# Attention scores over 64 rows, with a PSUM bank for each head

## The chip, the cores and the metric

The kernel runs on one core of one Trainium2 chip. The metric is device time in microseconds (us). Three runs of the kernel before took 2879.69, 2884.32 and 2884.14 us; their median is 2884.14 us.

## The reference

Two layers of a backbone with 256 context tokens and 512 main tokens of width 1024. Each layer normalizes and modulates the tokens, projects them with `w_in`, passes the columns through four mixers of 256 channels each, gates and merges these, and ends in a mixture of experts. In the second layer the context tokens get no output. The change is in three of the mixers; each has 4 heads of 64 channels. Their cores, cut:

```python
# retention, in chunks of 128 tokens, in two directions
scores = einsum('bnihd,bnjhd->bnhij', qc, kc) * intra
o_intra = einsum('bnhij,bnjhe->bnihe', scores, vc)
o_cross = einsum('bnihd,hi,nbhde->bnihe', qc, q_dec, s_prev)

# neighborhood attention: blocks of 128 queries against 256 nearby and 256 context keys, one softmax
# window attention (GQA): blocks of 128 queries against up to 384 nearby and 256 context keys
s_w = where(valid, einsum('bqkgd,bskd->bkgqs', qb, kb), NEG)
s_c = einsum('bqkgd,bckd->bkgqc', qb, kc)
prob = softmax_with_sink(concatenate([s_w, s_c], -1), sink)
```

So every score is a sum over the 64 channels of one head.

## The kernel before

Tokens stand in tiles of 128 on the partitions. The large products (`product`, L560 to L562) are three fp32r matmuls for each 128 rows of weights (high times high, high times low, low times high), and their weights are streamed from memory and split by ScalarE (L436) and VectorE (L437). The mixers are Python generators. `tick` steps them from inside the large products, so that their instructions lie between those of the projections and gates; within that, the scheduler of the tile framework sets the order on each engine, and each engine then works through its list in that order. A mixer must be done when the merge comes to it (`finish`).

A pair p holds two heads, one in channels 0 to 63 and one in channels 64 to 127. Queries and keys are transposed so that the channels lie on the partitions. `pad_halves` (L640) evacuates the transposed queries twice: ScalarE writes head 0 into the lower half of one buffer (L653), VectorE head 1 into the upper half of another (L654), and GpSimd has filled the other halves with zeros (L643, L644). With these zeros a score is one matmul over all 128 rows of `kT`, and the other head's channels count nothing. The fp32 matmuls appear in the trace as two records each.

- `retention`: for each of 20 chunks (6 tiles and 4 tiles of the two layers, two pairs each) one matmul makes both heads' scores (L738, 256 columns), two the products with the state (L741, 128 columns each). VectorE applies mask and decay to both heads at once (L744, L746), adds the directions (L748), and two matmuls follow (L751), then the sum (L753).
- `ctx_attention`: 8 steps of the first layer; both heads' scores (L859) share one PSUM bank.
- `neighborhood`: 16 steps; for head 0 the window (L909) and the context scores (L910), the bias (L911), then the same for head 1.
- `gqa`: 16 steps; L984 makes the scores of 256 or 384 window keys, L987 the context scores, head after head. Where 384 + 256 columns exceed a bank of 512 (half of the steps) the context scores of both heads share a third bank.
- `attend` is what follows the scores in each of these 40 attention steps: the maxima (L794 or L799, L802), the exponentials with their sums (L809, and L812 for a sink), the reciprocal of the sum (L819), the scaling (L820 on ScalarE for head 0, L821 on VectorE for head 1), the transposes of the probabilities (L824), their evacuation (L830) and the products with the values (L841). L841 writes 64 output columns for each head, head 0 to the lower and head 1 to the upper partitions.

PSUM has 8 banks in four pools: `mm` 2, `sc` 3, `tr` 2, `mod` 1. Scores take `sc`; the transposes and L841 take `tr`.

Of the kernel before, what the change touches and what calls it, by code (L numbers as in the profile page):

```python
# [9 lines left out]
F32 = mybir.dt.float32  # L10
# [3 lines left out]
AF = mybir.ActivationFunctionType  # L14
OP = mybir.AluOpType
# [4 lines left out]
NCTX = 256  # L20
# [284 lines left out]
class Prog:  # L305
# [333 lines left out]

    def pad_halves(self, dst, scale, blocks=False):  # L640


        self.nc.gpsimd.memset(dst[0][64:128], 0.0)  # L643
        self.nc.gpsimd.memset(dst[1][0:64], 0.0)  # L644

        def f(ps, sl):
            lo, up = (scale, scale) if isinstance(scale, float) else (scale[0:64], scale[64:128])
            i0, i1 = ps[0:64], ps[64:128]
            o0, o1 = dst[0][0:64, sl], dst[1][64:128, sl]
            if blocks and sl.start >= NCTX:  # L650
                i0, i1 = (x.rearrange("p (r j c) -> p r j c", j=4, c=16) for x in (i0, i1))
                o0, o1 = (x.rearrange("p (j r c) -> p r j c", j=4, c=16) for x in (o0, o1))
            self.nc.scalar.activation(o0, i0, AF.Copy, scale=lo)  # L653
            self.nc.vector.tensor_scalar(o1, i1, up, None, op0=OP.mult)  # L654
        return f
# [30 lines left out]
    def retention(self, l, tiles, store):  # L686
# [4 lines left out]
        for p in range(2):  # L691
# [36 lines left out]
            self.rope(rq)  # L728
            qp = self.buf(128, 2, NTOK)
            evac = self.pad_halves([qp.v[:, h] for h in range(2)], 0.125)  # L730
            yield
# [24 lines left out]
            for b in (kT, qp, S):  # L756
                b.free()
# [91 lines left out]

    def ctx_attention(self, p, qp, kT, value, store, sink):  # L850

        nc = self.nc
        for t in range(2):
            sl = slice(t * 128, t * 128 + 128)

            def scores():
                sc = self.ps_sc.tile([128, 2, 256], F32, name="sc")
                for h in range(2):
                    nc.tensor.matmul(sc[:, h], qp[h][:, sl], kT.v[:, :NCTX], start=True, stop=True)  # L859
                return [[sc[:, h]] for h in range(2)]  # L860
            yield from self.attend(scores, lambda h, k: value(h, k),
                                   lambda yo: nc.scalar.dma_start(store[p * 128 : p * 128 + 128, sl], yo), sink)

    def neighborhood(self, l, tiles, store):
# [7 lines left out]
        for p in range(2):  # L872
# [15 lines left out]
            self.head_norm(nq.v)  # L888
            qs = [self.buf_old(128, NTOK) for _ in range(2)]
            qp = [b.v for b in qs]  # L890
            evac = self.pad_halves(qp, gain[:, 0:1], blocks=True)
            yield
# [3 lines left out]
            if t0 == 0:  # L896
                yield from self.ctx_attention(p, qp, kT, lambda h, k: nv.v[:, k, h * 64 : h * 64 + 64], store, None)
            for j in range(4):
# [5 lines left out]
                def scores():  # L904
                    out = []
                    for h in range(2):
                        q = qp[h][:, NCTX + j * 128 : NCTX + j * 128 + 128]
                        sc = self.ps_sc.tile([128, 512], F32, name="sc")
# [3 lines left out]
                        out.append([sc])  # L912
                    return out

# [7 lines left out]
                yield from self.attend(scores, value, put)  # L922
            for b in (nv, kT, *qs, vw):
                b.free()

    def gqa(self, l, tiles, store):
# [19 lines left out]
        for p in range(2):  # L946
# [13 lines left out]
            self.rope(q)  # L960
            qs = [self.buf_old(128, NTOK) for _ in range(2)]
            qp = [b.v for b in qs]
            evac = self.pad_halves(qp, 1.0)
            yield
# [5 lines left out]
            if t0 == 0:  # L970
                yield from self.ctx_attention(p, qp, kT, lambda h, k: val(k), store, sk)
            for n in range(4):
# [3 lines left out]

                def scores():
                    own = w + NCTX > 512
                    rest = self.ps_sc.tile([128, 2, 256], F32, name="sc") if own else None
                    out = []  # L980
                    for h in range(2):
                        qh = qp[h][:, sl]
                        sc = self.ps_sc.tile([128, 512], F32, name="sc")
                        nc.tensor.matmul(sc[:, :w], qh, kT.v[:, (keys[0] + 2) * 128 : (keys[-1] + 3) * 128],  # L984
                                         start=True, stop=True)
                        r = rest[:, h] if own else sc[:, w : w + NCTX]
                        nc.tensor.matmul(r, qh, kT.v[:, :NCTX], start=True, stop=True)  # L987
                        for i, m in enumerate(keys):
                            if m != n:
                                b = sc[:, i * 128 : i * 128 + 128]  # L990
                                nc.vector.tensor_tensor(b, b, self.c("band_l" if m < n else "band_r"), op=OP.add)
                        out.append([sc[:, :w], r] if own else [sc[:, : w + NCTX]])
# [6 lines left out]
            for b in (kT, *qs):  # L999
                b.free()  # L1000
# [1260 lines left out]
```

## Time and profile before

| | |
|---|---|
| median of three runs | 2884.14 us |
| the profiled execution | 2886.01 us, its span 2884.2 us |
| TensorE matmul busy | 2695.0 us (93%) |
| VectorE, ScalarE, GpSimd busy | 2080.1, 1462.2, 654.0 us |
| mean granted TensorE clock | 0.972 |
| where the mixers' scores lie in the span | first layer 339 to 722 us, second layer 1725 to 2092 us |

Busy time of TensorE includes the tail of each matmul that overlaps with the next one, so matmul durations are not added up; the distance from one start to the next is what a matmul costs in a stream. The gap from the profiled execution's 2886.01 us to its span is 1.8 us.

### The profile page before, as it was taken

The page shows a single profiled execution, that of the slowest core. Times are in us where ns is not written, and L with a number is a line of the kernel's source. Part 1 is how long each engine was busy: PE and PEld are TensorE (multiplying, and loading weights), DVE is VectorE, ACT ScalarE, POOL GpSimd, SP SyncE. Part 2 cuts the span into 40 slices and gives each one's busy share as a digit, 9 for nine tenths or more (in the row PEclk, how much of TensorE's full clock was granted, in tenths as well). Part 3 has the DMA queues.
Part 4 walks back from the last instruction along what each step waited for, and adds up shares of the span by engine and source line. Part 5 has one row for each costly group of instructions (what it writes and reads, how often), then busy time and mean ns, then how long its engine had stood idle before and what let it go on. Part 6 is the DMA issues. An engine that isn't in the chain of part 4 may idle for free. (4 is left out here: it accounts for less than half of the span.)

```text
span 2884.2 us, 39086 instructions
## 1 busy us (share of the span) xinstructions
PE 2695.0 (93%) x13190; PEld 1807.1 (63%) x13190; DVE 2080.1 (72%) x3921; ACT 1462.2 (51%) x2219; POOL 654.0 (23%) x596
## 2 busy tenths in 40 slices
PE   5999999999999699999997789999999699999998
PEld 2767666667678456666554467778788455555444
DVE  6754454647345989998886668755845999998887
ACT  4322342432132478887776434432233477776665
POOL 2231111001001441221111321021101543323332
PEclk8999999999999799999999899999999799999999
DMA  8687445243535799999997865365435899999994
GB/s 275 197 250 234 146 127 182 88 135 102 169 123 184 266 331 375 370 353 352 370 366 244 279 204 171 115 203 165 131 128 158 272 362 371 376 365 330 347 352 131
DMA packets 268646, 699.37 MB, mean 242 GB/s; under 512 B 64836, under 2 KB 83512, under 8 KB 268440
## 3 DMA queue, kind: packets, MB, share of 16 engines
q1 hardware_dynamic: 170672, 531.30, 51.8%
q0 software_dynamic: 39744, 113.86, 14.7%
q10 hardware_dynamic: 58024, 51.65, 5.7%
q8 instruction: 106, 1.74, 0.2%
q14 instruction: 100, 0.82, 0.1%
HBM read 622.48 MB, written 80.44 MB: 244 GB/s over the span
## 5 line engine op out<-in xcount | busy, mean ns | idle before, releaser
L437 DVE TENSOR_TENSOR big_r<-big,big_r 128x1024 fp32r<-128x1024 f32 x512 | 613.6, 1221 | 76.1 <-ACT big_r L436 69.0
L436 ACT CAST big_r<-big 128x1024 fp32r<-128x1024 f32 x517 | 532.5, 1051 | 150.6 <-PE mm L562 74.0
L560 PE MATMUL mm<-big_r,turned 128*128 128x512 f32 x1248 | 514.4, 412 | 10.3 <-ACT turned L436 6.6
L561 PE MATMUL mm<-big_r,turned 128*128 128x512 f32 x1248 | 504.7, 404 | 1.6 <-DVE big_r L437 1.5
L562 PE MATMUL mm<-big_r,turned 128*128 128x512 f32 x1248 | 504.5, 404 | 0.0
L437 DVE TENSOR_TENSOR big_r<-raw,big_r 128x1024 fp32r<-128x1024 f32 x392 | 464.0, 1216 | 41.4 <-ACT big_r L436 35.5
L436 ACT CAST big_r<-raw 128x1024 fp32r<-128x1024 f32 x395 | 402.9, 1049 | 66.6 <-PE sc L562 36.0
L561 PE MATMUL sc<-big_r 128*72 128x512 f32 (+1 forms) x1024 | 409.7, 400 | 19.6 <-DVE big_r L437 19.0
L560 PE MATMUL sc<-big_r 128*72 128x512 f32 (+1 forms) x1024 | 407.0, 398 | 0.0
L562 PE MATMUL sc<-big_r 128*72 128x512 f32 (+1 forms) x1024 | 404.9, 395 | 0.0
L560 PEld LDWEIGHTS mm<-big_r,turned 128*128 128x128 f32 x1248 | 236.9, 190 | 110.3 <-issue 41.1
L562 PEld LDWEIGHTS mm<-big_r,turned 128*128 128x128 f32 x1248 | 236.8, 190 | 57.3 <-issue 8.1
L561 PEld LDWEIGHTS mm<-big_r,turned 128*128 128x128 f32 x1248 | 237.3, 190 | 54.3 <-issue 6.5
L561 PEld LDWEIGHTS sc<-big_r 128*72 128x72 f32 (+1 forms) x1024 | 138.4, 135 | 139.0 <-DVE big_r L437 55.7
L1897 POOL DMA_INDIRECT out_dram<-big x32 | 162.2, 5068 | 266.2 <-DVE big L1874 261.9
L1866 PE MATMUL mm<-big_r 128*72 128x512 f32 (+1 forms) x512 | 204.0, 398 | 0.4 <-DVE big_r L437 0.2
L560 PEld LDWEIGHTS sc<-big_r 128*72 128x72 f32 (+1 forms) x1024 | 139.1, 136 | 100.7 <-ACT big_r L436 7.7
L1867 PE MATMUL mm<-big_r 128*72 128x512 f32 (+1 forms) x512 | 201.5, 393 | 0.0
L562 PEld LDWEIGHTS sc<-big_r 128*72 128x72 f32 (+1 forms) x1024 | 138.8, 136 | 85.6 <-issue 1.0
L1865 PE MATMUL mm<-big_r 128*72 128x512 f32 (+1 forms) x512 | 184.5, 394 | 1.1 <-DVE big L1874 0.6
L1382 ACT ACTIVATE wa<-mm 128x512 f32<-128x512 f32 x80 | 47.7, 596 | 239.9 <-PE mm L562 239.6
L1368 DVE SCALAR_TENSOR_TENSOR wa<-wa,mm 128x512 f32<-128x512 f32 x60 | 41.1, 685 | 147.2 <-PE mm L562 141.5
(381 smaller groups left out, 3794.0 us busy)
## 6 DMA issues: line engine op xcount, KB each, us to landing
big<-in_exp_w_dram SPq DMA_DIRECT2D x393, 512.0 KB, 7.5
raw<-in_exp_w_dram SPq DMA_DIRECT2D x375, 512.0 KB, 7.2
big<-in_mod_w_dram SPq DMA_DIRECT2D x96, 512.0 KB, 4.6
big<-in_w_in_dram SPq DMA_DIRECT2D x68, 512.0 KB, 5.5
big<-in_w_in_dram SPq DMA_DIRECT2D x48, 256.0 KB, 5.5
big<-s_wc POOLq DMA_DIRECT2D x16, 576.0 KB, 6.2
big<-s_ph POOLq DMA_DIRECT2D x16, 388.0 KB, 4.4
big<-s_wb POOLq DMA_DIRECT2D x16, 384.0 KB, 3.8
```

What stands on the lines that cost most here:

```text
L436: return (self.nc.scalar.copy(hi, src), (v or self.nc.vector).tensor_tensor(lo, src, hi.bitcast(F32), op=OP.subtract))
L437: (v or self.nc.vector).tensor_tensor(lo, src, hi.bitcast(F32), op=OP.subtract))
L560: nc.tensor.matmul(ps, ah, wh, start=(k == 0), stop=False)
L561: nc.tensor.matmul(ps, ah, wl, start=False, stop=False)
L562: nc.tensor.matmul(ps, al, wh, start=False, stop=(k == n - 1))
L1368: nc.vector.scalar_tensor_tensor(tg, tg, 1.0, pb, op0=OP.add, op1=OP.mult)
L1382: nc.scalar.activation(tg, pg, AF.Tanh, scale=0.5)
L1865: nc.tensor.matmul(o, hh.v[:, k, :n], w[:, 0, half], start=(k == 0), stop=False)
L1866: nc.tensor.matmul(o, hh.v[:, k, :n], w[:, 1, half], start=False, stop=False)
L1867: nc.tensor.matmul(o, hl.v[:, k, :n], w[:, 0, half], start=False, stop=(k == 3))
L1897: scatter = lambda y, i: nc.gpsimd.indirect_dma_start(out=ya, out_offset=bass.IndirectOffsetOnAxis(ap=i, axis=0), in_=y, in_offset=None, b ...
```

## The change

`turned_rows` takes the place of `pad_halves`: each evacuation writes both heads in one instruction, in turn by ScalarE and VectorE, into one buffer, and nothing is zeroed. Each score matmul contracts over the 64 rows of its own head, in the lower or the upper half of TensorE's rows, and each head has its own PSUM bank. Scores of the two heads are issued alternately. In retention, VectorE's two operations on both heads become four on one head each. In `gqa` with 384 window keys the context scores of head 1 go to a bank of `tr`.

```diff
+    def turned_rows(self, dst, scale, blocks=False):
+        n = [0]
         def f(ps, sl):
-            lo, up = (scale, scale) if isinstance(scale, float) else (scale[0:64], scale[64:128])
-            i0, i1 = ps[0:64], ps[64:128]
-            o0, o1 = dst[0][0:64, sl], dst[1][64:128, sl]
+            i, o = ps, dst[:, sl]
...
-            self.nc.scalar.activation(o0, i0, AF.Copy, scale=lo)
-            self.nc.vector.tensor_scalar(o1, i1, up, None, op0=OP.mult)
+            n[0] += 1
+            if n[0] % 2:
+                self.nc.scalar.activation(o, i, AF.Copy, scale=scale)
+            else:
+                self.nc.vector.tensor_scalar(o, i, scale, None, op0=OP.mult)
@@ retention
-                sc = self.ps_sc.tile([128, 2, 128], F32, name="sc")
-                nc.tensor.matmul(sc, kT.v[:, sl], qp.v[:, :, sl], start=True, stop=True)
-                cr = self.ps_sc.tile([128, 2, 2, 64], F32, name="sc")
-                for h in range(2):
-                    nc.tensor.matmul(cr[:, h], qp.v[:, h, sl], S.v[:, n], start=True, stop=True)
...
-                nc.vector.tensor_tensor(sm, sc, m.v[:, hs], op=OP.mult)
-                nc.vector.tensor_tensor(t1, cr, qd[:, hs, :, None].to_broadcast([128, 2, 2, 64]), op=OP.mult)
+                bank = [self.ps_sc.tile([128, 2, 128], F32, name="sc") for _ in range(2)]
+                for h in range(2):
+                    r = slice(64 * h, 64 * h + 64)
+                    nc.tensor.matmul(bank[h][:, 0], kT.v[r, sl], qT.v[r, sl], start=True, stop=True)
+                for h in range(2):
+                    r = slice(64 * h, 64 * h + 64)
+                    nc.tensor.matmul(bank[h][:, 1], qT.v[r, sl], S.v[r, n], start=True, stop=True)
+                for h in range(2):
+                    nc.vector.tensor_tensor(sm[:, h], bank[h][:, 0], m.v[:, 2 * p + h], op=OP.mult)
+                    nc.vector.tensor_tensor(t1[:, h], bank[h][:, 1].rearrange("p (d e) -> p d e", d=2),
+                                            qd[:, 2 * p + h, :, None].to_broadcast([128, 2, 64]), op=OP.mult)
@@ ctx_attention
-                sc = self.ps_sc.tile([128, 2, 256], F32, name="sc")
+                sc = [self.ps_sc.tile([128, 512], F32, name="sc") for _ in range(2)]
                 for h in range(2):
-                    nc.tensor.matmul(sc[:, h], qp[h][:, sl], kT.v[:, :NCTX], start=True, stop=True)
+                    r = slice(64 * h, 64 * h + 64)
+                    nc.tensor.matmul(sc[h][:, :NCTX], qT.v[r, sl], kT.v[r, :NCTX], start=True, stop=True)
@@ neighborhood
-                    for h in range(2):
-                        nc.tensor.matmul(sc[:, :256], q, kk, start=True, stop=True)
-                        nc.tensor.matmul(sc[:, 256:], q, kT.v[:, :NCTX], start=True, stop=True)
-                        nc.vector.tensor_tensor(sc[:, :256], sc[:, :256], bias[:, h], op=OP.add)
+                    for h, r in enumerate(rows):
+                        nc.tensor.matmul(out[h][:, :256], q[r], kk[r], start=True, stop=True)
+                    for h, r in enumerate(rows):
+                        nc.tensor.matmul(out[h][:, 256:], q[r], kT.v[r, :NCTX], start=True, stop=True)
+                    for h in range(2):
+                        nc.vector.tensor_tensor(out[h][:, :256], out[h][:, :256], bias[:, h], op=OP.add)
@@ gqa
-                    rest = self.ps_sc.tile([128, 2, 256], F32, name="sc") if own else None
+                    sc = [self.ps_sc.tile([128, 512], F32, name="sc") for _ in range(2)]
+                    if not own:
+                        rest = [x[:, w : w + NCTX] for x in sc]
+                    else:
+                        rest = [self.ps_sc.tile([128, 512], F32, name="sc")[:, :NCTX],
+                                self.ps_tr.tile([128, 512], F32, name="tr")[:, :NCTX]]
...
+                    for h, r in enumerate(rows):
+                        nc.tensor.matmul(sc[h][:, :w], qT.v[r, sl], kT.v[r, (keys[0] + 2) * 128 : (keys[-1] + 3) * 128],
+                                         start=True, stop=True)
+                    for h, r in enumerate(rows):
+                        nc.tensor.matmul(rest[h], qT.v[r, sl], kT.v[r, :NCTX], start=True, stop=True)
```

In the changed file the scores are L744 and L747 (retention), L865 (context), L915 and L917 (neighborhood) and L994 and L997 (`gqa`); the transposes L824 become L829, L841 becomes L846 and L751 becomes L756.

The order of the instructions moves with it. On TensorE, in the first layer's first neighborhood steps, before (the number behind a name is the buffer; `sc_2710` is head 0's scores, `sc_2714` head 1's):

```order
L824 MATMUL tr_2677<-cst_81,big_80 128x128 x2
L824 MATMUL tr_2681<-cst_81,big_80 128x128 x2
L909 MATMUL sc_2710<-big_80 128x256
L910 MATMUL sc_2710<-big_80 128x256
L841 MATMUL tr_2691<-big_80 64x128 x4
L909 MATMUL sc_2714<-big_80 128x256
L910 MATMUL sc_2714<-big_80 128x256
L560 MATMUL mm_2730<-big_r_79 128x512
```

And with the change (`sc_2708` is head 0's scores, `sc_2709` head 1's):

```order
L846 MATMUL tr_2689<-big_80 64x128 x4
L561 MATMUL mm_2640<-big_r_79,turned_362 128x512
L562 MATMUL mm_2640<-big_r_79,turned_362 128x512
L915 MATMUL sc_2708<-big_80 128x256
L915 MATMUL sc_2709<-big_80 128x256
L917 MATMUL sc_2708<-big_80 128x256
L917 MATMUL sc_2709<-big_80 128x256
L560 MATMUL mm_2728<-big_r_79 128x512
```

The four score matmuls, which stood in two pieces around L841, now stand together, between large products.

On TensorE in the second layer's `gqa`, second pair, third step, before (`sc_14866` is that step's last score tile; `tr_14797` takes the transposed probabilities of the step before it):

```order
L984 MATMUL sc_14866<-big_80 128x384
L561 MATMUL mm_15009<-big_r_79,turned_12291 128x512
L562 MATMUL mm_15009<-big_r_79,turned_12291 128x512
L560 MATMUL mm_15064<-big_r_79,turned_12303 128x512
L561 MATMUL mm_15064<-big_r_79,turned_12303 128x512
L562 MATMUL mm_15064<-big_r_79,turned_12303 128x512
L560 MATMUL mm_15064<-big_r_79,turned_12303 128x512
L561 MATMUL mm_15064<-big_r_79,turned_12303 128x512
L562 MATMUL mm_15064<-big_r_79,turned_12303 128x512
L560 MATMUL mm_15064<-big_r_79,turned_12303 128x512
L561 MATMUL mm_15064<-big_r_79,turned_12303 128x512
L824 MATMUL tr_14797<-cst_81,big_80 128x128 x4
```

And with the change (`tr_14769` is head 1's context scores of the second step, `sc_14875` to `sc_14877` the scores of the third; `tr_14812` takes the second step's transposed probabilities):

```order
L829 MATMUL tr_14736<-cst_81,big_80 128x128 x4
L846 MATMUL tr_14748<-big_80 64x128 x8
L997 MATMUL tr_14769<-big_80 128x256
L994 MATMUL sc_14875<-big_80 128x384
L994 MATMUL sc_14876<-big_80 128x384
L997 MATMUL sc_14877<-big_80 128x256
L829 MATMUL tr_14812<-cst_81,big_80 128x128 x4
```

Head 1's context scores of the second step now stand behind L846 of the first step, and between them and the transposes of the same step there is no large product any more, where before there were 23 behind that step's last score tile.

On TensorE in retention, one chunk of the first layer, before (`sc_5078` both heads' scores):

```order
L738 MATMUL sc_5078<-big_80 128x256
L741 MATMUL sc_5080<-big_80 128x128 x2
L560 MATMUL mm_5093<-big_r_79,turned_358 128x512
L561 MATMUL mm_5093<-big_r_79,turned_358 128x512
L562 MATMUL mm_5093<-big_r_79,turned_358 128x512
L751 MATMUL sc_5087<-big_80,sa_5083 128x128 x2
```

And with the change (`sc_5071` is head 0's bank, `sc_5072` head 1's):

```order
L744 MATMUL sc_5071<-big_80 128x128
L744 MATMUL sc_5072<-big_80 128x128
L747 MATMUL sc_5071<-big_80 128x128
L747 MATMUL sc_5072<-big_80 128x128
L560 MATMUL mm_5088<-big_r_79,turned_358 128x512
L561 MATMUL mm_5088<-big_r_79,turned_358 128x512
L756 MATMUL sc_5082<-big_80,sa_5070 128x128
L562 MATMUL mm_5088<-big_r_79,turned_358 128x512
L756 MATMUL sc_5082<-big_80,sa_5070 128x128
```

The pair of L751 is taken apart, with a large product between its two heads.

## Rows read from the trace of the kernel before

**Rows 1.** Windows: span, busy us (instructions) of each engine, TensorE clock, DMA share, GB/s

```profile
330.00:500.00 170.00, 167.95 (x840) 116.02 (x839) 83.16 (x184) 62.50 (x129) 26.02 (x33) 1.00 0.47 141
560.00:700.00 140.00, 137.32 (x695) 97.34 (x694) 80.44 (x196) 46.82 (x107) 11.58 (x17) 1.00 0.37 112
...
1800.00:1910.00 110.00, 108.18 (x645) 84.41 (x644) 77.38 (x221) 53.31 (x128) 11.98 (x17) 1.00 0.47 139
```

**Rows 2.** Lines by shape, score matmuls: records, busy us, mean ns, idle before

```profile
L909 PE MATMUL sc<-big 128*128 128x256 f32 x64 | 19.7, 389 | 0.1
...
L984 PE MATMUL sc<-big 128*128 128x384 f32 x32 | 13.4, 499 | 0.0
...
L741 PE MATMUL sc<-big 128*128 128x128 f32 x80 | 12.1, 274 | 0.0
```

**Rows 3.** Timeline of TensorE, a neighborhood step: start us, duration us, group of records

```profile
352.06 0.60 PE L909 MATMUL sc<-big 128*128 128x256 f32 x2
352.50 0.59 PE L910 MATMUL sc<-big 128*128 128x256 f32 x2
353.02 0.66 PE L841 MATMUL tr<-big 128*64 128x128 f32 x8
353.61 0.70 PE L909 MATMUL sc<-big 128*128 128x256 f32 x2
354.15 0.59 PE L910 MATMUL sc<-big 128*128 128x256 f32 x2
```

**Rows 4.** Timeline of TensorE, a chunk of retention, to the next large product

```profile
661.30 0.61 PE L741 MATMUL sc<-big 128*128 128x128 f32 x4
661.67 0.48 PE L560 MATMUL mm<-big_r,turned 128*128 128x512 f32 x1
661.99 0.39 PE L561 MATMUL mm<-big_r,turned 128*128 128x512 f32 x1
```

**Rows 5.** Timeline of TensorE, experts of layer one: transposes with 72 rows

```profile
1007.80 0.40 PE L562 MATMUL sc<-big_r 128*72 128x512 f32 x1
1008.04 0.42 PE L1827 MATMUL tr<-cst,big 72*128 72x72 f32 x4
```

**Rows 6.** Timeline of TensorE, experts of layer two: transposes with 56 rows

```profile
2300.64 0.39 PE L561 MATMUL sc<-big_r 128*56 128x512 f32 x1
2300.87 0.40 PE L562 MATMUL sc<-big_r 128*56 128x512 f32 x1
2301.20 0.45 PE L1827 MATMUL tr<-cst,big 56*128 56x56 f32 x4
```

**Rows 7.** Lines by shape, from the last score to the scaled probabilities of `gqa`

```profile
L809 ACT ACTIVATION_READ_ACCUMULATOR big<-sc,sm_neg 128x1 f32 x96 | 19.0, 198 | 0.0
L809 ACT ACTIVATE big<-sc,sm_neg 128x256 f32<-128x256 f32 x32 | 15.0, 469 | 6.6 <-DVE sm_neg L794 4.6 <-DVE sm_neg L802 1.5 <-ACT att_y L844 0.5
...
L812 ACT ACTIVATE sm_sum<-gqa_sink,sm_neg 128x1 f32<-128x1 f32 x40 | 11.7, 291 | 0.0
...
L799 DVE TENSOR_REDUCE sm_max<-sc 128x1 f32<-128x256 f32 x24 | 9.5, 414 | 6.5 <-PE sc L859 5.1 <-PE sc L987 1.4
L809 ACT ACTIVATE big<-sc,sm_neg 128x384 f32<-128x384 f32 x16 | 9.3, 582 | 6.4 <-DVE sm_neg L802 6.1 <-issue 0.2
...
L820 ACT ACTIVATE big<-big,sm_rc 128x640 f32<-128x640 f32 x8 | 6.6, 829 | 9.5 <-DVE sm_rc L819 3.9 <-DVE sm_max L799 3.6 <-DVE big L821 1.9
```

**Rows 8.** The same of L815: durations min/median/max in ns, first and last start

```profile
L815 DVE TENSOR_REDUCE sm_tot<-sm_sum x20: 136/149/161, 504.8 to 1897.9; 128x2 f32<-128x4 f32 x12, 128x2 f32<-128x6 f32 x8
```

**Rows 9.** Lines by shape: weight loads of L984, and what they waited for

```profile
L984 PEld LDWEIGHTS sc<-big 128*128 128x128 f32 x64 | 11.4, 189 | 4.8 <-POOL big L643 1.5 <-ACT big L809 1.0 <-issue 0.9
```

**Rows 10.** Lines by shape: retention's VectorE operations, and L751's weight loads

```profile
L751 PEld LDWEIGHTS sc<-big,sa 128*128 128x128 f32 x80 | 10.8, 190 | 3.7 <-DVE sa L744 2.3 <-DVE sa L748 0.8
...
L744 DVE TENSOR_TENSOR sa<-sc,big 128x256 f32<-128x256 f32 x20 | 8.5, 424 | 8.1 <-PE sc L738 7.4
...
L748 DVE TENSOR_TENSOR sa<-sa 128x128 f32<-128x128 f32 x20 | 5.8, 289 | 0.4
```

More of the change, by code (lines that the diff above doesn't have):

```diff
@@ L728, in retention @@
             self.rope(rq)
-            qp = self.buf(128, 2, NTOK)
-            evac = self.pad_halves([qp.v[:, h] for h in range(2)], 0.125)
+            qT = self.buf(128, NTOK)
+            evac = self.turned_rows(qT.v, 0.125)
             yield
@@ L755, in retention @@
                 yield
-            for b in (kT, qp, S):
+            for b in (kT, qT, S):
                 b.free()
@@ L848, in attend, with ctx_attention @@
         yield
-    def ctx_attention(self, p, qp, kT, value, store, sink):
+    def ctx_attention(self, p, qT, kT, value, store, sink):
         nc = self.nc
@@ L856, in scores @@
             def scores():
[L857 removed]
+                sc = [self.ps_sc.tile([128, 512], F32, name="sc") for _ in range(2)]
                 for h in range(2):
[L859 to L860 removed]
+                    r = slice(64 * h, 64 * h + 64)
+                    nc.tensor.matmul(sc[h][:, :NCTX], qT.v[r, sl], kT.v[r, :NCTX], start=True, stop=True)
+                return [[x[:, :NCTX]] for x in sc]
             yield from self.attend(scores, lambda h, k: value(h, k),
@@ L888, in neighborhood @@
             self.head_norm(nq.v)
-            qs = [self.buf_old(128, NTOK) for _ in range(2)]
-            qp = [b.v for b in qs]
-            evac = self.pad_halves(qp, gain[:, 0:1], blocks=True)
+            qT = self.buf_old(128, NTOK)
+            evac = self.turned_rows(qT.v, gain[:, 0:1], blocks=True)
             yield
@@ L896, in neighborhood @@
             if t0 == 0:
-                yield from self.ctx_attention(p, qp, kT, lambda h, k: nv.v[:, k, h * 64 : h * 64 + 64], store, None)
+                yield from self.ctx_attention(p, qT, kT, lambda h, k: nv.v[:, k, h * 64 : h * 64 + 64], store, None)
             for j in range(4):
@@ L904, in scores @@
                 def scores():
-                    out = []
-                    for h in range(2):
-                        q = qp[h][:, NCTX + j * 128 : NCTX + j * 128 + 128]
-                        sc = self.ps_sc.tile([128, 512], F32, name="sc")
-                        nc.tensor.matmul(sc[:, :256], q, kk, start=True, stop=True)
-                        nc.tensor.matmul(sc[:, 256:], q, kT.v[:, :NCTX], start=True, stop=True)
-                        nc.vector.tensor_tensor(sc[:, :256], sc[:, :256], bias[:, h], op=OP.add)
-                        out.append([sc])
-                    return out
+                    out = [self.ps_sc.tile([128, 512], F32, name="sc") for _ in range(2)]
+                    rows = [slice(64 * h, 64 * h + 64) for h in range(2)]
+                    q = qT.v[:, NCTX + j * 128 : NCTX + j * 128 + 128]
+                    for h, r in enumerate(rows):
+                        nc.tensor.matmul(out[h][:, :256], q[r], kk[r], start=True, stop=True)
+                    for h, r in enumerate(rows):
+                        nc.tensor.matmul(out[h][:, 256:], q[r], kT.v[r, :NCTX], start=True, stop=True)
+                    for h in range(2):
+                        nc.vector.tensor_tensor(out[h][:, :256], out[h][:, :256], bias[:, h], op=OP.add)
+                    return [[x] for x in out]
                 def value(h, k):
@@ L922, in neighborhood @@
                 yield from self.attend(scores, value, put)
-            for b in (nv, kT, *qs, vw):
+            for b in (nv, kT, qT, vw):
                 b.free()
@@ L960, in gqa @@
             self.rope(q)
-            qs = [self.buf_old(128, NTOK) for _ in range(2)]
-            qp = [b.v for b in qs]
-            evac = self.pad_halves(qp, 1.0)
+            qT = self.buf_old(128, NTOK)
+            evac = self.turned_rows(qT.v, 1.0)
             yield
@@ L970, in gqa @@
             if t0 == 0:
-                yield from self.ctx_attention(p, qp, kT, lambda h, k: val(k), store, sk)
+                yield from self.ctx_attention(p, qT, kT, lambda h, k: val(k), store, sk)
             for n in range(4):
@@ L978, in scores @@
                     own = w + NCTX > 512
-                    rest = self.ps_sc.tile([128, 2, 256], F32, name="sc") if own else None
+                    sc = [self.ps_sc.tile([128, 512], F32, name="sc") for _ in range(2)]
[4 more added lines that the diff above has]
+                                self.ps_tr.tile([128, 512], F32, name="tr")[:, :NCTX]]
+                    rows = [slice(64 * h, 64 * h + 64) for h in range(2)]
+                    for h, r in enumerate(rows):
[3 more added lines that the diff above has]
+                        nc.tensor.matmul(rest[h], qT.v[r, sl], kT.v[r, :NCTX], start=True, stop=True)
                     out = []
                     for h in range(2):
[L982 to L987, printed above, removed]
                         for i, m in enumerate(keys):
                             if m != n:
-                                b = sc[:, i * 128 : i * 128 + 128]
+                                b = sc[h][:, i * 128 : i * 128 + 128]
                                 nc.vector.tensor_tensor(b, b, self.c("band_l" if m < n else "band_r"), op=OP.add)
-                        out.append([sc[:, :w], r] if own else [sc[:, : w + NCTX]])
+                        out.append([sc[h][:, :w], rest[h]] if own else [sc[h][:, : w + NCTX]])
                     return out
@@ L998, in gqa @@
                                        lambda yo: nc.scalar.dma_start(store[p * 128 : p * 128 + 128, sl], yo), sk)
-            for b in (kT, *qs):
+            for b in (kT, qT):
                 b.free()
```

7 lines of the change are left out of this document (2 added, 5 removed).

## The prediction

> **What bounds the kernel now.** I read the windows of the three stages with scores first [rows 1]: TensorE is busy 167.95 of 170, 137.32 of 140 and 108.18 of 110 us at full clock, while VectorE is at 49 to 70%, ScalarE below that, and the DMA share is 0.37 to 0.47. So here a microsecond more or less in TensorE's list is one in the time, and what the other engines do counts only where TensorE comes to an instruction whose input is not there. Then I read the timeline of TensorE for what a matmul costs in the stream. Two records of 256 columns take 0.44 us (352.06 to 352.50) [rows 3], so 0.22 each; by their columns a record of 384 is 0.33 and one of 128 is 0.11. The last agrees with retention: the large product after four such records starts at 661.67 but needs 0.32 us where 0.23 are usual [rows 4], so it began at about 661.76, and four records took 0.46 [rows 4]. A large matmul takes 0.23 (2300.64 to 2300.87) [rows 6].
>
> **Streaming saved.** Before, the scores are 64 records each of L909, L910 and L987, 32 of L859, 40 of L738 and 32 of L984 with 256 columns, 32 of L984 with 384 and 80 of L741 with 128 (the kinds in [rows 2]): 296 x 0.22 + 32 x 0.33 + 80 x 0.11 = 84.5 us. After, the same columns stream; what can be saved is the overlap of the two heads, one in each half of the rows. The trace of before shows such an overlap for halves of the columns: L841's eight records, two heads of four, start at 353.02 and the next group starts at 353.61 [rows 3]; one after the other they would need 0.88, in pairs 0.44, and the gap is 0.59. I take full overlap. But the order has not put all pairs side by side. I counted 100 unbroken runs of score matmuls in TensorE's order with the change; 49 of them hold one head alone (22.7 us of records, nothing saved), 51 hold both (61.8 us of records, 35.0 if the longer head of each run counts). Saved: 26.8 us. The bounds are 0 (no overlap of row halves, which no row of before shows) and 84.5/2 = 42.
>
> "TensorE: Matmul & The Clock Gate" of the Trainium skill (Part 3, measured speedup) gives 3.07 for four row tiles, about three quarters of the ideal. By that the 61.8 us would become 40 instead of 35 and the time 2903; no row here shows a pair of row halves.
>
> **Switches added.** Around L841 the array's shape changes, from 128 rows by 128 columns to two halves of the columns and back. From L910 at 352.50 to the next L910 at 354.15 are 1.65 us [rows 3]; the work in it is 0.44 (L910) + 0.44 (L841 in pairs) + 0.44 (L909) = 1.32. So one switch there and one back cost 0.33 us. The second is the dearer one: the L909 behind it needs 0.54 to the next group where 0.44 is usual, 0.10 of weight load that nothing hides, and there is 0.10 more before it; so about 0.20 into a shape with 128 columns, 0.13 into L841's 64. The expert stage says the same of rows: in layer one, where the transposes have 72 rows, L1827 starts 0.24 behind the matmul before it, as a large one would [rows 5]; in layer two, with 56 rows, 0.33 behind, 0.10 more [rows 6]. I read that as the price of going to half the rows (there the columns change too).
>
> "TensorEngine Tiling (Array Packing)" of the Trainium skill (Key Properties) says that a change of the tiling mode, not of the tile, drains TensorE. By it each run of score matmuls pays on entering and on leaving; the trace agrees for L841 with its 0.33 us for both [rows 3].
>
> In the order, changes of shape (outside the experts) rise from 327 to 471. Into full shape or into the row halves there are 148 more, at 0.20 each 29.6 us; into L841 6 fewer (its pieces are broken up less), at 0.13 0.8 us less; 2 more into the narrow shapes of L483 and L1201, 0.2 us. Sum: 29.0 us. The bounds: 0, if row halves need no switch at all, and 148 x 0.33 = 49.
>
> **Waits from the new order.** In `gqa` with 384 window keys, head 1's context scores now sit in a `tr` bank and come last, and everything up to the scaling needs both heads. From there to the transposes it takes one maximum of 0.41 (L799), for each head exponentials of 0.58 and 0.47 with two sums of 0.20 and the sink's 0.29, and a scaling of 0.83 [rows 7], and three small VectorE operations of about 0.15 like L815 [rows 8]: 0.41 + 2 x 1.74 + 0.83 + 0.45 = 5.2 us. TensorE waits for what of this its own list doesn't cover. In the second layer's second pair the order leaves, between tr_14769 and the transposes of its step, only two matmuls of 384 columns side by side (0.66 us) and one of 256, partly beside them: 0.9 us. The step after it looks the same: 2 x (5.2 - 0.9) = 8.6 us, where before 23 and 47 large products (5 and 11 us) stood behind those steps' last score tiles. In the first layer the four such steps have 12, 18, 14 and 15 large products of 0.23 and some small ones, 3.6, 4.5, 4.1 and 4.5 us, where 5.2 are needed: 1.6 + 0.7 + 1.1 + 0.7 = 4.1. Sum: 12.7 us. The bounds are 0 (a wait that is taken out of another wait) and the same chain bare in all 8 steps, 8 x 5.2 = 42. What queues behind a waiting transpose is everything on TensorE, the large products too, so no other work fills it.
>
> **What I take at little or nothing.** The fills with zeros go; L984's weight loads waited 1.5 us for one [rows 9]: -1.5. GpSimd's time itself is beside the path. The 18 pairs of query evacuations become 18 single ones of the same length; they lie beside large products, so I take 0, bounded by 18 operations of some 0.5 us (the nearest row is L809 with 256 columns, 0.47 [rows 7]), -9 to 0. In retention two VectorE operations of 0.42 become four of about 0.29 (L748 is one of 128 columns) [rows 10], 0.31 more in each of 20 chunks. L751 waited 2.3 us for L744 in all [rows 10]. Now head 0's L751 needs one operation of 0.29 and has two large products ahead of it; head 1's needs three, 0.87, and has three and head 0's pair ahead, 0.9. So 0, bounded by -2.3 and 20 x (0.87 - 0.42) = 9.
>
> **Sum.** -26.8 + 29.0 + 12.7 - 1.5 = +13.4 us on the profiled execution's 2886.0, so 2899.4; the median of the runs lies 1.9 below that execution, so 2897.5 us. Nothing later gives it back: the stages behind are bound by TensorE or by the streamed weights, and these start where the mixers end.
>
> **Rivals.** What this kernel's measurement can tell from no change is about 0.2%, 5.8 us.
> - The waits are hidden. The scheduler has put large products elsewhere, and what waits at a transpose may be taken out of waits that stand now, of which the same stages have some (TensorE idles 2 us of each 110 to 170 even by busy time [rows 1]). Then -26.8 + 29.0 - 1.5 = +0.7: 2884.8. Against it: two steps have nothing to cover them. 0.18.
> - The other side, faster: a switch to row halves is cheap. It decides from a switch of (26.8 + 1.5 - 12.7 - 5.8)/148 = 0.066 us; at no cost the sum is -15.6, 2868.5, and with half of that price 2873. For it speaks that no row shows a switch of rows alone; against it the 0.10 of [rows 5, 6] and the load of 0.10 behind any switch [rows 3]. 0.12.
> - The halves of the rows don't overlap; each head streams after the other, and the switches are paid for nothing. 29.0 + 12.7 - 1.5 = +40.2: 2924. L841's pairs speak against it [rows 3]. 0.08.
>
> **How the numbers follow.** The forecast has 0.62, with its own range of 2890 to 2912 (a wait in only half of the steps; overlap of three quarters and 0.25 for a switch). All of it and the last rival are slower by over 0.2%: 0.70. The first rival is within 0.2%: 0.18. The second is faster: 0.12. The range leaves out the last rival and most of the second: 2880 to 2916.
>
> **What would show it.** In the timeline of the changed kernel a run of L915, L915, L917, L917 should take about 0.9 us, with head 1's records starting right behind head 0's, some 0.1 us of idle array before the run and before the large product behind it. If L917 starts 0.9 us behind the first L915, the rows don't overlap. L829's weight loads should show waits of some 4 us, twice, in the second layer's `gqa`, and together about 10 us more than L824's now. The window 1800 to 1910 should lose most time, the first layer's retention next to none. If the neighborhood's part gets shorter by as much as `gqa` loses, I have priced the switches too high.

## The result, and the profile after

The changed kernel took 2912.34 us (median of four runs, 2911.06 to 2915.88), the kernel before 2884.23 beside it: a ratio of 1.0102, interval 1.0085 to 1.0120. So it is slower, by 28 us where I had forecast 13; the time lies inside the range, and the sum is short by 15 us. The profiled execution has a span of 2909.7 us, 25.5 more than before.

Where the 25.5 us arise is read from one line that both kernels run twice, right behind the mixers (the transposes of the merged rows, L1409 before, L1421 after; first and last start in the span):

```profile
L1409 PE MATMUL tr<-cst,big x80: 270/272/300, 834.2 to 2196.6; 128*128 128x128 f32 x80
```

```profile
L1421 PE MATMUL tr<-cst,big x80: 270/272/301, 836.9 to 2222.2; 128*128 128x128 f32 x80
```

At the end of the first layer's mixers the changed kernel is 2.7 us late, at the end of the second's 25.6. The windows of the changed kernel (columns as in [rows 1]) narrow it down:

```profile
330.00:500.00 170.00, 165.35 (x840) 107.96 (x839) 81.73 (x189) 61.62 (x134) 22.95 (x29) 0.99 0.47 138
560.00:700.00 140.00, 138.30 (x704) 92.80 (x703) 79.49 (x205) 46.04 (x105) 9.17 (x14) 1.00 0.36 112
...
1800.00:1885.00 85.00, 83.42 (x473) 62.37 (x472) 59.69 (x159) 39.22 (x87) 3.20 (x4) 1.00 0.49 149
1885.00:1920.00 35.00, 25.41 (x134) 17.63 (x135) 15.42 (x48) 14.91 (x41) 1.50 (x2) 0.76 0.15 46
```

The first layer's windows are nearly as busy as those of [rows 1] (165.35 us where 167.95 were, and 138.30 where 137.32 were). From 1885 to 1920 us TensorE works 25.4 of 35 us, and the granted clock is 0.76 there: part of that stretch runs at the lower of the two levels, 1.2 GHz. Before, the window from 1800 to 1910 had 108.18 of 110 us at full clock [rows 1]. The timeline of TensorE in that stretch (a group's duration, then the idle time before it and what ended it):

```profile
1890.22 0.40 PE L562 MATMUL mm<-big_r,turned 128*128 128x512 f32 x1
1890.46 1.03 PE L829 MATMUL tr<-cst,big 128*128 128x128 f32 x8
1891.78 1.58 PE L846 MATMUL tr<-big 128*64 128x128 f32 x16 [0.29 <-ACT big L835]
1893.29 0.70 PE L997 MATMUL tr<-big 64*128 64x256 f32 x2
1895.40 2.10 PE L994 MATMUL sc<-big 64*128 64x384 f32 x4 [1.41 <-ACT big L814]
1896.71 1.11 PE L997 MATMUL sc<-big 64*128 64x256 f32 x2
1899.61 2.54 PE L829 MATMUL tr<-cst,big 128*128 128x128 f32 x10 [1.79 <-ACT big L825]
1902.36 2.40 PE L846 MATMUL tr<-big 128*64 128x128 f32 x20 [0.22 <-DVE big L835]
1904.69 2.45 PE L1213 MATMUL tr<-big 128*16 128x128 f32 x16
1907.07 0.70 PE L997 MATMUL tr<-big 64*128 64x256 f32 x2
1910.67 0.94 PE L994 MATMUL sc<-big 64*128 64x256 f32 x3 [2.90 <-ACT big L814]
...
1915.17 1.97 PE L829 MATMUL tr<-cst,big 128*128 128x128 f32 x8 [2.91 <-ACT big L825]
1916.79 0.78 PE L560 MATMUL mm<-big_r 128*128 128x512 f32 x1
```

Between the large products at 1890.22 and 1916.79 there is none: two steps of the second layer's second pair of `gqa` stand bare. TensorE waits twice for scaled probabilities (L825), as predicted, and twice more for the exponentials (L814) before the next step's window scores can start, because the step holds all three banks of `sc`. The 20 records of L846 at 1902.36 take 2.40 us, nearly twice what they need at full clock (1.31, a row below).

The stretch is not all of it. The two kernels have the same large products in the same number, so one can be compared with its counterpart: the one at 1916.79 is 17.4 us late, the one at 2016.9 is 25.4 us late. So some 8 us more are lost behind the stretch. There TensorE waits more often for the loads and the VectorE work of the fourth mixer (`s5`, which the change does not touch); the waits of TensorE from 1931 to 2062, and before from 1903 to 2040 (us, times, longest):

```profile
PE sc L1292 <- DMA big<-s_tp: 3.7, 3, 1.9
PE sc L1296 <- DVE big L1233: 1.4, 1, 1.4
PE sc L1269 <- DMA big<-s_wb: 1.1, 1, 1.1
```

```profile
PE mm L560 <- ACT wa L1382: 2.6, 4, 1.1
PE sc L1280 <- DMA big<-s_tp: 2.2, 1, 2.2
```

With the smaller ones these waits add up to 9.4 us, and before to 5.2. What delays that mixer is not shown.

Why no large product is left there is seen on the other engines. The queries of that pair go through a load on GpSimd's queue (L593) and VectorE's normalization (the product with the gain is L939 before and L946 after). Before, from the timelines of GpSimd and VectorE:

```profile
1792.60 0.80 POOL L593 DMA_DIRECT2D big<-pE_d  x1 [9.92 <-ACT att_y L844]
```

```profile
1821.17 0.69 DVE L939 TENSOR_TENSOR big<-big,gqa_gain 128x512 f32<-128x512 f32 x1
```

After:

```profile
1864.95 0.77 POOL L593 DMA_DIRECT2D big<-pE_d  x1 [39.16 <-ACT att_y L849]
```

```profile
1877.93 0.69 DVE L946 TENSOR_TENSOR big<-big,gqa_gain 128x512 f32<-128x512 f32 x1
```

Before, the load issued at 1792.6 us, and the queries were normalized 42 us ahead of that pair's first score at 1863.2. After, GpSimd sits idle for 39 us until the first pair's last output is copied out (L849), and the pair's scores start at 1883.1, as soon as the queries are there. Between the transposes of that pair's keys and of its queries TensorE's list has 51 large products, where it had none; they are used up while the queries are on their way, and are missing 20 us later.

What makes the load late is memory. `buf_old` gives out the free piece that was freed longest ago. The second pair's queries get word 5440 of the large tile in both kernels. With one query buffer instead of two the pieces given out earlier shift, and in the changed kernel the first pair's last step has head 0's probabilities at 5440; before, these lay at 15904.

### The profile page after: what moved, and what is told of

The parts are those of the page before. It is cut to its first block, busy times and chain, and to the rows that moved or that the text cites. A ratio compares the mean times of both kernels' runs of the same rounds, so it can differ in the third digit from the quotient of the medians.

```text
span 2909.7 us, 39157 instructions
## 1 busy us (share of the span) xinstructions
PE 2704.3 (93%) x13230; PEld 1789.4 (61%) x13230; DVE 2072.9 (71%) x3949; ACT 1461.3 (50%) x2213; POOL 635.1 (22%) x572
## 5 line engine op out<-in xcount | busy, mean ns | idle before, releaser
L560 PE MATMUL mm<-big_r,turned 128*128 128x512 f32 x1248 | 512.6, 411 | 8.0 <-ACT turned L436 7.2
L561 PE MATMUL mm<-big_r,turned 128*128 128x512 f32 x1248 | 504.2, 404 | 2.7 <-DVE big_r L437 2.7
L562 PE MATMUL mm<-big_r,turned 128*128 128x512 f32 x1248 | 504.2, 404 | 0.0
L437 DVE TENSOR_TENSOR big_r<-raw,big_r 128x1024 fp32r<-128x1024 f32 x392 | 464.1, 1217 | 39.3 <-ACT big_r L436 32.0
L561 PE MATMUL sc<-big_r 128*72 128x512 f32 (+1 forms) x1024 | 410.0, 400 | 19.5 <-DVE big_r L437 18.4
L560 PE MATMUL sc<-big_r 128*72 128x512 f32 (+1 forms) x1024 | 407.4, 398 | 0.0
L562 PE MATMUL sc<-big_r 128*72 128x512 f32 (+1 forms) x1024 | 405.2, 396 | 0.0
L560 PEld LDWEIGHTS mm<-big_r,turned 128*128 128x128 f32 x1248 | 237.0, 190 | 111.9 <-issue 47.9
L562 PEld LDWEIGHTS mm<-big_r,turned 128*128 128x128 f32 x1248 | 237.1, 190 | 59.3 <-issue 10.6
L561 PEld LDWEIGHTS mm<-big_r,turned 128*128 128x128 f32 x1248 | 237.4, 190 | 56.7 <-issue 7.5
L561 PEld LDWEIGHTS sc<-big_r 128*72 128x72 f32 (+1 forms) x1024 | 138.4, 135 | 139.1 <-DVE big_r L437 55.0
L560 PEld LDWEIGHTS sc<-big_r 128*72 128x72 f32 (+1 forms) x1024 | 139.1, 136 | 100.8 <-ACT big_r L436 7.7
L562 PEld LDWEIGHTS sc<-big_r 128*72 128x72 f32 (+1 forms) x1024 | 138.9, 136 | 85.8 <-issue 1.2
```

Of the source, the lines that this page charges most:

```text
L437: (v or self.nc.vector).tensor_tensor(lo, src, hi.bitcast(F32), op=OP.subtract))
L560: nc.tensor.matmul(ps, ah, wh, start=(k == 0), stop=False)
L561: nc.tensor.matmul(ps, ah, wl, start=False, stop=False)
L562: nc.tensor.matmul(ps, al, wh, start=False, stop=(k == n - 1))
```

## The experiments

Theory M: this late load is what the sum lacks; the sum's own terms are about right. Theory C: the waits belong to the steps with 384 window keys and their banks, and I sized their chain too small. Each run is compared with the kernel before on the same chip; us are the ratio's share of 2884.

**The memory as before.** A second query buffer that nothing uses, in all three mixers:

```diff
-            qT = self.buf_old(128, NTOK)
+            qT, spare = [self.buf_old(128, NTOK) for _ in range(2)]
```

> The changed kernel, with a second query buffer in each of the three mixers that nothing reads or writes, so that every other buffer lies where it lay before. Theory M: in the second layer's gqa the changed kernel loads the second pair's queries into memory that the first pair's last probabilities occupied; the load (L593) issues at 1865 us instead of 1793, and the large products are used up before that pair's steps. Then here the load issues 60 to 75 us before that pair's scores again, and the kernel takes 2892 to 2898 us, some 15 to 19 less than the changed kernel's 2912. Theory C (the prediction's): the waits are those of the steps with 384 window keys themselves, with their banks, wherever the load is: 2908 to 2914.

Measured: 2892.54 us, ratio 1.0031 (1.0019 to 1.0043), 9 us slower than before where the changed kernel is 29. Its profiled execution took 2901.51 us; there the granted clock was 0.72 from 2050 to 2080 us, and the median is used. The load issues at 1791.6 us, and the queries are normalized at 1816:

```profile
1816.08 0.68 DVE L946 TENSOR_TENSOR big<-big,gqa_gain 128x512 f32<-128x512 f32 x1
```

The same 20 records of L846 then run at full clock:

```profile
1887.27 1.31 PE L846 MATMUL tr<-big 128*64 128x128 f32 x20
```

Theory M holds: 20 us go with an edit that only changes where buffers lie.

**The same buffer in one mixer.** As above, in `neighborhood` alone, and in `gqa` alone.

> The changed kernel with the unused second query buffer in neighborhood attention alone (two lines). In the list of TensorE the second pair of the second layer's gqa then follows the first at once, five large products after its first query transposes, where the changed kernel has 51 in between. Theory M (where the queries are loaded decides): the load issues 60 to 75 us before the pair's scores and the kernel takes 2889 to 2897 us, as e1_memory. Theory C (the chain of the steps with 384 window keys and their banks): 2908 to 2914.

> The same unused buffer in gqa alone: as much memory, but the second pair's queries still land on memory of the first pair's last probabilities (51 large products in between, as in the changed kernel). Theory M: no gain, 2908 to 2915 us. If a buffer more helps for another reason (fewer waits for memory anywhere in gqa): 2892 to 2900.

Measured: 2891.58 us, ratio 1.0020 (1.0011 to 1.0029) in `neighborhood`; 2909.68 us, ratio 1.0092 (1.0076 to 1.0109) in `gqa`. As much memory is added in both; what differs is where later buffers land. The queries are normalized at

```profile
1861.79 0.69 DVE L946 TENSOR_TENSOR big<-big,gqa_gain 128x512 f32<-128x512 f32 x1
```

in the first (pair's first score at 1870.4) and at

```profile
1873.44 0.69 DVE L946 TENSOR_TENSOR big<-big,gqa_gain 128x512 f32<-128x512 f32 x1
```

in the second (1878.6). Theory M is right on both times. On one detail the expectation was wrong: in the first the load issues at 1848.9, only 21 us ahead of the scores and 16 earlier than in the changed kernel. That lets the pair follow the first while large products are left, but not to its end: in that trace, of an execution that took 2898.21 us, the pair's last steps stand bare, with no large product from 1899.46 to 1912.40.

The longest time from one large product to the next around the second pair is, in the traces, 26.6 us in the changed kernel, 25.3 with the buffer in `gqa`, 12.9 with it in `neighborhood`, 5.6 with the memory as before and 4.3 in the kernel before.

**The kernel before, with the late load.** The second pair's queries and keys put on the first pair's last probabilities:

```diff
+        self.last_pr = [b.o for b in pb]
...
-            q = self.rows_of(l, "E", 256 + p * 128, 128, tiles)
+            q = self.rows_of(l, "E", 256 + p * 128, 128, tiles, self.last_pr[0] if p and t0 else None)
```

> The kernel before, with the second pair's queries and keys of the second layer's gqa put on the memory of the first pair's last probabilities. Theory M: the load issues some 50 to 70 us later, the second pair starts 30 large products later and its last step but one stands bare: 4 to 10 us more than before, 2888 to 2894. Theory C: within 3 us of before.

Measured: 2889.63 us, ratio 1.0017 (1.0008 to 1.0027), 5 us slower. The load issues at 1858.9 instead of 1792.6. So the late load costs by itself, but a quarter of what it costs in the changed kernel: the pair starts 10 us later than before, not 20, and its list leaves one step bare instead of two (8.2 us without a large product).

**No row halves, the rest as in the run with the memory as before.** Each score over 128 rows with padded queries; a bank for each head and the new order of issue stay.

```diff
-                    nc.tensor.matmul(sc[h][:, :NCTX], qT.v[r, sl], kT.v[r, :NCTX], start=True, stop=True)
+                    nc.tensor.matmul(sc[h][:, :NCTX], qT[h].v[:, sl], kT.v[:, :NCTX], start=True, stop=True)
```

> Memory and PSUM banks as in e1_memory, and scores issued in the same order, but each over all 128 rows with padded queries: no halves of the rows, so no overlap and no switches for them (326 changes of array shape instead of 472). By the prediction's terms overlap (25 us here) and switches (146 x 0.20 = 29) nearly cancel: 1 to 5 us less than e1_memory. If a switch is cheap (0.1), 10 us more than e1_memory; if it is dear (0.3), 18 less.

Measured: 2893.93 us, ratio 1.0042 (1.0029 to 1.0056). It is 3 us slower than with row halves rather than 1 to 5 faster; the two intervals overlap. So overlap and switches cancel within what can be measured. By elimination, the 9 to 12 us that remain come from what both kernels share: the banks, the order that follows from them, and retention's four VectorE operations. Which of these, and which waits, is not shown.

**One mixer at a time**, memory as before.

> The change in gqa alone, with its steps on context, on memory as before. By the prediction's terms: overlap 9.4 us saved, 50 more changes of array shape 10.0 us, and the waits of the steps with 384 window keys 5 to 10 us, since each of them takes all three score banks and a bank of the transposes: 2889 to 2895 us. If these waits are hidden: 2882 to 2886.

> The change in neighborhood attention alone, with its two steps on context; gqa and retention as before, memory as before. Overlap saves 10.2 us, the changes of array shape rise by 29 (5.8 us), and no step needs a third bank: 4 us less than before, 2880. If a switch costs 0.3 or the halves do not overlap: no change or slower, 2883 to 2893.

> The change in retention alone, memory as before. By the prediction's terms: the overlap saves 5.8 us, 58 changes of array shape more cost 11.6, the four VectorE operations in place of two nothing: 5.8 us more than before, 2890. If a switch to row halves is cheap (0.1 or less): 2884 or less. If VectorE's two more operations in each chunk come onto the path (20 x 0.45 us): 2899.

Measured: `gqa` 2892.5 us, ratio 1.0022 (1.0011 to 1.0032), +6 us; neighborhood attention 2882.31 us, 0.9995 (0.9985 to 1.0005), -1 us; retention 2888.68 us, 1.0027 (1.0016 to 1.0037), +8 us. Expected were +5 to +10, -4 and +6. The sum of the parts, +13, agrees with the +9 of all together as far as the intervals go. By the terms, retention pays most for its switches: its runs are short, 58 more changes of shape for 5.8 us of overlap. Its run agrees with that sum, but does not tell the switches from the rest of the edit.

**The price of a switch without row halves.** The kernel before, with the value products issued for head 1 first; head 1's probabilities are evacuated last, so a group stands in one piece.

```diff
-            for h in range(2):
+            for h in (1, 0):
                 nc.tensor.matmul(yt[64 * h : 64 * h + 64], values(h, k), pr[h][:, k * 128 : k * 128 + 128],
```

> The kernel before with one word changed: the products with the values (L841) are issued for head 1 first. Head 1's probabilities are evacuated after head 0's, so the first of the group waits for both and the group stands in one piece on TensorE's list: 286 changes of array shape instead of 331, no row halves anywhere. By the prediction's 0.33 us for a switch there and one back: 22 pairs, 7 us less than before, 2877. If the switches cost little, or the later start of the group costs as much: within 3 us of before.

Measured: 2877.32 us, ratio 0.9984 (0.9974 to 0.9993): 5 us less than before for 45 switches, 0.10 each (0.04 to 0.17), where 0.165 were forecast, at the edge of the interval. This is a net price, since the group also starts later.

**Row halves where they stay together.** Neighborhood attention and its context steps alone; there head 1's window scores first, the other three behind it with priority:

```diff
-                    for h, r in enumerate(rows):
-                        nc.tensor.matmul(out[h][:, :256], q[r], kk[r], start=True, stop=True)
+                    first = nc.tensor.matmul(out[1][:, :256], q[rows[1]], kk[rows[1]], start=True, stop=True)
+                    with self.after(first), self.tc.high_priority(2000):
+                        nc.tensor.matmul(out[0][:, :256], q[rows[0]], kk[rows[0]], start=True, stop=True)
```

> As e13_na_run_values, with the values' products in their old order: overlap saves 12.8 us, 22 changes of array shape more than before cost 4.4: 8 us less than before, 2876. If what e4_na lost against its forecast (3 us) is a wait that comes with the banks: 2880.

> A version put together from the findings: row halves in neighborhood attention and its steps on context only, as e4_na; there head 1's window scores first and the other three score matmuls behind it with priority, so that 19 runs hold 14.1 of 15.4 parts of the streaming with both heads; and the values' products with head 1 first, as e9_values. Overlap saves 12.4 us, 322 changes of array shape instead of 331 save 2 more: 14 us less than before, 2870. If the waits that come with a bank for each head eat it, as in gqa: 2880 or more.

Measured: 2875.4 us, ratio 0.9978 (0.9968 to 0.9987), -6 us; with the value products in one piece 2868.14 us, ratio 0.9950 (0.9935 to 0.9965), -14 us; -8 and -14 were forecast. This version beats both kernels. In its timeline a step's eight records form one run, both heads 10 ns apart:

```profile
348.91 0.48 PE L942 MATMUL sc<-big 64*128 64x256 f32 x1
348.92 0.48 PE L944 MATMUL sc<-big 64*128 64x256 f32 x1
349.23 0.38 PE L942 MATMUL sc<-big 64*128 64x256 f32 x1
349.24 0.38 PE L944 MATMUL sc<-big 64*128 64x256 f32 x1
349.45 0.60 PE L946 MATMUL sc<-big 64*128 64x256 f32 x4
349.98 0.50 PE L560 MATMUL mm<-big_r 128*128 128x512 f32 x1
```

From 348.91 to 349.98 are 1.07 us; one after the other the eight records (0.215 each) would stream for 1.72.

**One block for a run.** Another way to keep a run together, in the first layer:

```diff
+                    with ExitStack() if t0 else self.tc.tile_critical():
```

> As e1_memory, but in the first layer the score matmuls of both heads of a step of retention, of neighborhood attention and of the steps on context are put on TensorE's list as one block (28 to 44 blocks), so that no run there holds one head alone. By the prediction's terms: overlap saves 5 us more than in e1_memory, 24 changes of array shape fewer save 5 more: 2882 us. Against it: each block is jumped to and from, which no run has priced; at 0.25 us a block the gain is gone, at 0.5 us it is 10 us slower.

Measured: 2975.14 us, ratio 1.0296 (1.0271 to 1.0320), 85 us slower: a clear miss. The jump to a block and back was priced at 0.25 to 0.5 us. The timeline around one block:

```profile
355.06 0.45 PE L562 MATMUL mm<-big_r 128*128 128x512 f32 x1
357.37 1.13 PE L918 MATMUL sc<-big 64*128 64x256 f32 x4 [1.85 <-DMA y<-att_y]
358.28 1.07 PE L920 MATMUL sc<-big 64*128 64x256 f32 x4
359.44 0.79 PE L560 MATMUL mm<-big_r,turned 128*128 128x512 f32 x1
```

The block starts 2.3 us after the product before it, and runs at the low clock (1.13 us for the group that needs 0.70 at full clock). Over the first layer's 28 blocks the starts leave 39.3 us beyond streaming at the entries (0.6 to 5.2 each) and 12.5 at the exits: 52 of the 85 us. Whether the jump itself takes this time, or a wait that comes with a block, is not shown: at the block above the profile names the landing of a DMA. The rest I have not placed; the mean granted clock is 0.963, against 0.970 in the run with the memory as before.

## Why the prediction was right and wrong

The direction, the place of the largest loss and two of three terms were right; the third term had the wrong cause and left out the clock, and a part of the edit that I took at nothing was worth 20 us.

- **Streaming saved, 26.8 us: right.** The first run of the changed kernel's neighborhood steps:

```profile
347.73 0.40 PE L562 MATMUL mm<-big_r,turned 128*128 128x512 f32 x1
348.06 0.70 PE L915 MATMUL sc<-big 64*128 64x256 f32 x4
348.60 0.60 PE L917 MATMUL sc<-big 64*128 64x256 f32 x4
349.12 0.50 PE L560 MATMUL mm<-big_r 128*128 128x512 f32 x1
349.46 0.40 PE L561 MATMUL mm<-big_r 128*128 128x512 f32 x1
```

  From 348.06 to 349.12 are 1.06 us, of which 0.86 stream (about 0.9 was predicted for the run, with 0.1 idle before it and 0.1 behind), and head 1's records start 6 ns behind head 0's. Over all 100 runs, first start to last record, without the first weight load and two waits, the streaming fell from 82.8 to 59.2 us: 23.6 saved. With the 22.7 us of the runs of one head, full overlap would give 57.7 us; the 59.2 lie 1.5 above, and the other 1.7 us of the forecast were missing before the change (82.8 instead of 84.5). A run with both heads takes the time of one head plus 0.1. The speedup that "TensorE: Matmul & The Clock Gate" of the Trainium skill (Part 3, measured speedup) reports for four row tiles is three quarters of the ideal; as an estimate for two, this would have made 40 us of 61.8, and 62.7 us in all. The trace is 3.5 us below that.
- **Switches, 29.0 us: right in size.** In the trace L915 starts 0.33 behind the L562 that needs 0.23, its first load costs 0.11 more, and the same at the way back (0.34 from L560 to L561). Averaged over the trace an entry into row halves costs 0.205 and a return 0.186 us; all changes of shape together cost some 25 us more than before. "TensorEngine Tiling (Array Packing)" of the Trainium skill (Key Properties) says that a change of the tiling mode drains TensorE; the trace agrees as far as it shows it, with about 0.1 us of idle array on each side of a run. The difference of this term and the last is +1 to +2 us; +2.2 was forecast.
- **Waits from the new order, 12.7 us: the step that failed.** 8.6 us of it were for two bare steps of the second layer's second pair. The place was right, and the two waits for L825 are there (L829's loads wait 2.5 and 3.3 us, where I had said some 4). But I took the bare list as a property of those steps, when it came from the queries' late load, and priced only what waits at the transposes. From head 1's context scores to the transposes the trace has 6.3 us (1893.29 to 1899.61) and 8.1 (1907.07 to 1915.17), where the chain was summed to 5.2. Inside that time the weight loads wait 5.6 us before L994, for banks that the exponentials still read. The table of waits for weight loads, 1883 to 1920:

```profile
PEld tr L829 <- ACT big L825: 5.8, 2, 3.3
PEld sc L994 <- ACT big L814: 5.6, 4, 3.3
```

  TensorE itself idles 9.0 us before the four groups (1.41, 1.79, 2.90 and 2.91 in the timeline above). That this is near 8.6 is luck, since half of it is a wait that I had not priced. The stretch makes the kernel 14.7 us later (17.4, less the 2.7 of the first layer). The other 5.7 us are by estimate the clock's low level, which makes 1.31 us of L846 into 2.40 and which the sum left out; and some 8 us more follow behind the stretch, which it left out too.

  With the memory as before the kernel is 9 us slower, but that is not this term come true. Without the two bare steps the forecast is 13.4 - 8.6 = 4.8 us, just under the interval of that run (5.5 to 12.4); its trace still shows 3.5 us of L829's waits for L825 in the second layer.
- **What I took at nothing without a reason** is one buffer of queries instead of two. I costed the fills that went with the second buffer, and the evacuations, and never asked who gets the memory. With the memory as before 20 of the 29 us go (ratio 1.0031 instead of 1.0102); the two bare steps that I had put down to the new order are part of them.
- **The first layer** is 2.7 us later in all. L829's waits for L825 rise from 1.7 us (L824's for L820) to 5.6 there, by 3.9 where 4.1 were forecast; those of L846 for L835 rise too, from 6.2 (L841's for L830) to 10.5, which had no term. **Retention's VectorE operations** cost about 1 us on the path: L756 waits 3.4 us for L749 in all, L751 waited 2.3 for L744 [rows 10].
- **The rivals.** Hidden waits (2884.8) are out by the two waits for L825, cheap switches by the 0.205 and 0.186 us. That the halves don't overlap (2924) is out by the trace, though its time is nearer than mine to the measured one: a time alone would have chosen the wrong story.

## What to carry to other kernels

When an edit adds or drops a buffer in a memory that is handed out by age, look up which later load lands on which earlier tile, and what that load must wait for; the order of the engines shows it as work that moves far from the edit. Row halves paid here where both heads' products stand together in TensorE's list (a ratio of 0.9978 in neighborhood attention with runs kept together, 1.0027 in retention with its short ones): count the runs that hold both, and pay 0.2 us on each side of a run. To keep a group together, issue the member whose input comes last first; the runs that did so got faster (0.9984 and 0.9978), while a block for each run cost 1.9 us apiece.

## What the runs showed of the hardware beyond that

In the bare stretch, where TensorE waited between its groups, the granted clock fell to the lower level (0.53 from 1895 to 1905 us), and the matmuls took nearly twice as long (L846's group 2.40 us instead of 1.31): there the waits cost more than their own length. Entering a block of two or four score matmuls left TensorE idle for 0.6 to 5.2 us, whatever part of that is the jump.
